# Fewer, larger groups of small matrix products between the large ones

## The chip, the cores and the metric

One core of one Trainium2 chip runs the whole kernel, in one launch. The metric is the device time in microseconds (us). PE is TensorE (with PEld for its weight loads), DVE VectorE, ACT ScalarE, POOL GpSimd, SP SyncE, which issues most DMAs.

## The reference

One layer of a hybrid backbone over 640 tokens: 512 "latent" tokens on a grid and 128 "context" tokens, width 2048, float32.

```python
def _layer(x, mod, s0, shift_fn, lp):
    sh1, sc1, g1, sh2, sc2, g2 = jnp.split(mod, 6, axis=-1)       # mod = silu(c) @ w_mod + b_mod  (adaLN)
    h = _rmsnorm(x, lp['norm1_g']) * (1.0 + sc1) + sh1
    p = h @ lp['w_in']                                            # 2048 -> 5408 columns
    o_a, s_fin = _rwkv7_bidir(shift_fn(p[..., :C_SHIFT], lp['mu_shift']), s0, lp)
    o_b = _chunk_gmlp(jax.nn.gelu(p[..., C_SHIFT:]), lp)          # 8 groups of 128 columns
    x = x + g1 * (jnp.concatenate([o_a, o_b], axis=-1) @ lp['w_out'])
    h = _rmsnorm(x, lp['norm2_g']) * (1.0 + sc2) + sh2
    ff = (jax.nn.silu(h @ lp['w_ffn_gate']) * (h @ lp['w_ffn_up'])) @ lp['w_ffn_down']
    return x + g2 * ff, s_fin
```

`_rwkv7_bidir` runs, for 16 heads of 64 columns and for both directions, `S = S*w + (S a) b^T + v k^T; y = S r` over the tokens; the kernel does it in chunks of 64 tokens. `_chunk_gmlp` is, per group, a layer norm of one half and a 128x128 product over the tokens of a chunk, times the other half.

## The kernel before

Three stages follow one another. **The input stage** multiplies by `w_in` and prepares the recurrence; **the second stage** runs the recurrence over the chunks, with the output projection (`wout`, L1081 to L1083) as filler; **the third** is the feed-forward part. Only the input stage's code is touched.

Every float32 product of the large matrices is made of three products of rounded halves, of 128x320 outputs each: in `win` L194 (`h_hi`,`hi`), L195 (`h_lo`,`hi`) and L198 (`h_hi`,`lo`); below, "large products". The input stage walks over 43 blocks of 128 columns of `w_in`, four pieces of 24 large products to a block. `wide` counts eighths of a piece; twice in each half of a piece `between` lets three `Mixer` queues trace some of the small work, up to a budget that each `yield` of that work spends: `mixA` (the blocks' own work: `take_r`, `take_v`, `take_k` for a pair of heads; `take_gv`, `take_gu` for a gMLP group), `mixS` (`solve`, a 16x16 substitution on DVE) and `mixM` (`merge`, which joins the 16x16 inverses of a pair into 64x64 ones). A negative yield ends the budget, an integer holds the queue. After the last block the queues are drained, and then whatever is left of `mod_all`, the adaLN products. What is traced so is placed on each engine by a list scheduler; only the first and second stage's PE order is written by hand. Each engine runs its instructions in the order placed.

The small products, all in the input stage:
- in `take_k`'s `chunks`, once for each of 8 pairs and 2 directions: `pG` (L677) in three groups, then transposes `pXT` (L697) in groups of 8 and of 2 chunks, then `pW` (L711) in two groups of 5 chunks. `both(name)` hands out the two PSUM banks g0 and g1 of pool `pk`, one buffer each, so that a new group waits until ACT or DVE has copied out the one before.
- in `merge`, for each pair and direction: three `pblk` groups (L885, 32x32 tiles), `pM` (L910) and `pT` (L919), each of them copied out before the next. Their PSUM tiles come from `pt_`, which has two buffers.
- `pvt`, `pw` (transposes) and `psp` of a gMLP group or of `take_v`, full 128x128, from `pt_` too.
- `pm` (L948): the adaLN products, 2x512 outputs, four of them side by side in four column strips of the array; `mod_all` loads 2 MB of `w_mod`, uses them in two times four products, and so on for 32 loads. One `next(mods)` is taken 1.36 times per piece. `mod_cols` (L180, `ptm`) transposes a finished part. The loads, and the sum with the bias (`ms`), use one SBUF slot (`mraw`) in turn.

The second stage's first work is `o_load` (L1067 to L1069): SP loads `ol` from the gMLP outputs in DRAM (`d_o`), ACT casts it to `oh`, DVE subtracts. These tiles lie over the input stage's released SBUF.

Of the kernel before, what the change touches and what calls it, by code (L numbers as in the profile page):

```python
# [49 lines left out]
MODR = 1.36  # L50
# [39 lines left out]
def flow_step(ctx: ExitStack, tc, x_prompt, x_sample, state_rwkv, c, c_ctx, w_mod, b_mod,  # L90
# [456 lines left out]
    def take_v(pr, p):  # L547
        o = pairs[p]
        o.zv = bk.tile([P, T], F32, tag="zv", name="zv", bufs=1)
        yield from shifted(o.zv, pr, 16 + p)  # L550
        yield 1.5
        vt = bp.tile([P, NT, P], F32, tag="vt", name="vt", bufs=1)
        for (t0, t1) in ((0, 4), (4, 5)):
            ps = pt_.tile([P, 4, P], F32, tag="pt", name="pvt")
            for t in range(t0, t1):
                TE.transpose(ps[:, t - t0, :], o.zv[:, t * P:(t + 1) * P], ident)
            S.copy(vt[:, t0:t1, :], ps[:, 0:t1 - t0, :])
            yield 0.5
        nc.sync.dma_start(d_vt[p, 0].rearrange("(q t) v -> t q v", t=P), vt)
        nc.sync.dma_start(c3(d_vt[p, 1]), c3(d_vt[p, 0])[:, ::-1])  # L560

    def take_k(pr, p):
# [104 lines left out]
        def chunks(d):  # L667
# [7 lines left out]
            for (c0, c1) in ((0, 4), (4, 8), (8, NCH)):  # L675
# [4 lines left out]
                    for cc in range(c0, c1) for h in range(2)])  # L680
# [14 lines left out]
            for (c0, c1) in ((0, 8), (8, NCH)):  # L695
                two = [ps.rearrange("p (c t) -> p c t", t=CH) for ps in both("pXT")]
                in_turn([lambda cc=cc, h=h: TE.transpose(  # L697
                    two[h][:, cc - c0, :], X[hsl(h), cc].rearrange("p s t -> p (s t)"), ident[hsl(h), hsl(h)])
                    for cc in range(c0, c1) for h in range(2)])
                for h in range(2):  # L700
                    ps = two[h]
                    XT = bz.tile([P, 8, CH], F32, tag="XT", name="XT", bufs=2)
                    S.copy(XT[:, 0:c1 - c0, :], ps[:, 0:c1 - c0, :])
                    nc.sync.dma_start(d_S[p, :, d, c0:c1, F_X + CH * h:F_X + CH * h + CH], XT[:, 0:c1 - c0, :])
                yield 0.2 * (c1 - c0)
            two = [ps.rearrange("p (c t) -> p c t", t=CH) for ps in both("pW0")]
            for c0 in (0, 5):
                ps = two[c0 // 5][:, 0:5, :]
                for cc in range(c0, c0 + 5):
                    for h in range(2):  # L710
                        TE.matmul(ps[osl(h), cc - c0, :], GA[hsl(h), cc, :], Z[hsl(h), cc, h, :], start=True, stop=True)  # L711
                for h in range(2):
                    S.copy(Z[osl(h), c0:c0 + 5, h, :], ps[osl(h)])
                yield 1.0
# [45 lines left out]
    def take_gv(vv, g):  # L760
# [10 lines left out]
        for (t0, t1) in ((0, 4), (4, 5)):  # L771
            ps = pt_.tile([P, 4, P], F32, tag="pt", name="pvt2")
            for t in range(t0, t1):
                TE.transpose(ps[:, t - t0, :], vv[:, t * P:(t + 1) * P], ident)
            S.copy(vt[:, t0:t1, :], ps[:, 0:t1 - t0, :])
            yield 0.6
# [25 lines left out]
    def take_gu(uu, g):  # L802
# [5 lines left out]
        for (t0, t1) in ((0, 4), (4, 5)):  # L808
            ps = pt_.tile([P, 4, P], F32, tag="pt", name="psp")
            for t in range(t0, t1):  # L810
                TE.matmul(ps[:, t - t0, :], vt[:, t, :], wspT, start=True, stop=True)
# [50 lines left out]
    def merge(p, d2):  # L862

        GB = pairs[p].GB
        for gq in range(8):
# [8 lines left out]
        yield HOLD  # L874
        for d in range(2):
            GBd = GB[d]
            TF = bp.tile([P, NCH, CH], F32, tag="TF", name="TF")
            Tn, TT, A1 = TB[:, d, :, 0, :], TB[:, d, :, 1, :], A1_[:, d]

            def blk(lhs, rhs, rows=range(4)):  # L880
                ps = pt_.tile([P, NCH, 32], F32, tag="pt", name="pblk")
                for cc in range(NCH):
                    for a_ in rows:
                        s = slice(32 * a_, 32 * a_ + 32)
                        TE.matmul(ps[s, cc, :], lhs[s, cc, :], rhs[s, cc, :], start=True, stop=True,  # L885
                                  tile_position=(32 * a_, 32 * a_))
                return ps

            M1 = bp.tile([P, NCH, 32], F32, tag="M1", name="M1")
            yield -1.0  # L890
            ps = blk(A1, Tn)
            S.copy(M1, ps)
            yield 1.6
            yield -1.0

            ps = blk(TT, M1, (0, 2))
            for h in range(2):
                V.tensor_add(Tn[lo32(h)], ps[lo32(h)], Tn[lo32(h)])
            yield 1.6
            yield -1.0  # L900
            ps = blk(M1, TT)
            V.tensor_add(TF[:, :, 32:64], ps, TT)
            S.activation(TF[:, :, 0:32], TF[:, :, 32:64], AF.Copy, scale=mlo[:, 0:1])
            yield 1.7
            M2 = bp.tile([P, NCH, 32], F32, tag="M1", name="M2")
            yield -1.0
            ps = pt_.tile([P, NCH, 32], F32, tag="pt", name="pM2")
            for cc in range(NCH):
                for h in range(2):
                    TE.matmul(ps[hi32(h), cc, :], GBd[lo32(h), cc, 32:64], Tn[lo32(h), cc, :],  # L910
                              start=True, stop=True, tile_position=(64 * (1 - h), 64 * (1 - h) + 32))
            for h in range(2):
                S.copy(M2[hi32(h), :, :], ps[hi32(h), :, :])
            yield 1.2
            yield -1.0
            ps = pt_.tile([P, NCH, 32], F32, tag="pt", name="pT2")
            for cc in range(NCH):
                for h in range(2):
                    TE.matmul(ps[lo32(h), cc, :], M2[hi32(h), cc, :], TF[hi32(h), cc, 32:64],  # L919
                              start=True, stop=True, tile_position=(64 * (1 - h) + 32, 64 * (1 - h)))  # L920
            for h in range(2):
                S.copy(TF[lo32(h), :, 32:64], ps[lo32(h), :, :])
            yield 1.2
            BQ.dma_start(d_S[p, :, d, :, F_T:F_T + CH], TF)
            merged.append(p)
        G.memset(TB[:, :, :, 0, 0:16], 0.0)


# [10 lines left out]
    def mod_all():  # L939
        for g in (2, 4, 3, 5):  # L940
            pm = cur["psum"].tile([P, 512], F32, tag="pmod", name=f"pm{g}")
            quad = load_mod(g, 0)
            for _ in range(4):
                yield
            for kb in range(0, KB, 2):
                for u in range(2):
                    for j in range(4):
                        TE.matmul(pm[32 * j:32 * j + 2, :], cT[:, 2 * (kb + u):2 * (kb + u) + 2], quad[:, u, j, :],  # L948
                                  start=(kb + u == 0), stop=(kb + u == KB - 1), tile_position=(0, 32 * j))
                for _ in range(2):  # L950
                    yield
                if kb + 2 < KB:
                    quad = load_mod(g, kb + 2)
                    for _ in range(4):
                        yield
# [6 lines left out]
            yield  # L962
            yield
            for j in range(4):
                V.tensor_add(ms[32 * j:32 * j + 2, :], pm[32 * j:32 * j + 2, :], ms[32 * j:32 * j + 2, :])
            mod_cols(cur["tp"], ms, modc[g], tag=cur["tag"])
            yield
# [25 lines left out]
    mods = mod_all()  # L993
    due = 0.0
# [26 lines left out]
    for n, (b, q) in list(enumerate(pieces))[N0:]:  # L1021
# [6 lines left out]
        due += MODR  # L1028
        while due >= 1.0:
            due -= 1.0  # L1030
            next(mods, None)
# [3 lines left out]
    for _ in mods:  # L1035
        pass
# [1134 lines left out]
```

## Time and profile before

| | |
|---|---|
| time, median of 3 runs | 3188.06 us (3185.64 to 3188.2) |
| the profiled execution: its time / its span | 3182.42 us / 3180.6 us |
| PE, weight loads, DVE, ACT, POOL busy | 96%, 89%, 74%, 46%, 39% |
| input stage, first to last large product | 49.5 to 1062.9 us of the span |
| TensorE clock granted, mean | 0.993 |

A row of the timeline gives the start in us of the span, the time from the group's first start to its last end, the engine, the code line, what is written from what, the sizes and the count; in brackets the idle time ahead of it and what ended that. A float32 product outside `win` shows as two records. The input stage is the first third of the span.

### The profile page before, as it was taken

Reading aid. Unit: us, or ns where it says so; the run is one execution under the profiler, and the core shown is the slowest. Engines: PE = TensorE matmul, PEld = TensorE weight load, DVE = VectorE, ACT = ScalarE, POOL = GpSimd, SP = SyncE. Lnnn points to the kernel's source line nnn. Section 1 sums busy time; section 2 is a strip of 40 time slices with the busy share of each in tenths; the row PEclk is TensorE's granted clock in tenths of the full one; section 3 lists DMA queues with packets and bytes.
Section 4 is the critical chain, followed back from the end, with each engine's and each line's share of the span. In section 5 each row is a group of like instructions: output and inputs, shape, how many; then the busy total and the mean of one; then the engine's idle time right before and its main releaser. Section 6 shows DMA issues by size and latency. Waiting matters only on the chain.

```text
span 3180.6 us, 71623 instructions
## 1 busy us (share of the span) xinstructions
PE 3059.6 (96%) x27896; PEld 2844.7 (89%) x27896; DVE 2354.6 (74%) x4119; ACT 1474.4 (46%) x3216; POOL 1238.2 (39%) x1081
## 2 busy tenths in 40 slices
PE   6999999999999999999999999999999999999997
PEld 3788878788878888899999999999999999999997
DVE  4567777667776688767977777777777787888888
ACT  3344544544454444357544444444444454444365
POOL 2001121221122034411456665666656645555542
PEclk9999999999999999999999999999999999999999
DMA  9767786867777688575343434434343364554453
GB/s 371 249 190 201 213 233 175 218 196 203 210 208 202 205 285 275 157 221 155 110 132 107 121 118 127 122 107 127 119 122 119 109 200 150 159 167 123 135 163 123
DMA packets 740436, 550.84 MB, mean 173 GB/s; under 512 B 141056, under 2 KB 673504, under 8 KB 731264
## 3 DMA queue, kind: packets, MB, share of 16 engines
q1 hardware_dynamic: 727136, 532.47, 55.4%
q0 software_dynamic: 10624, 13.23, 1.8%
q8 instruction: 219, 3.59, 0.5%
q14 instruction: 121, 0.99, 0.1%
q10 hardware_dynamic: 2336, 0.57, 0.1%
HBM read 437.79 MB, written 110.95 MB: 173 GB/s over the span
## 4 chain that ended last, share of the span: by engine, by line
PE 45%; DVE 3%; issue 1%; DMA 1%; POOL 1%; ACT 0%; SPq 0%; DVEq 0%; POOLq 0%; ACTq 0%
PE P L1688 15%; PE P L1685 15%; PE P L1686 15%; DVE lo L1466 1%; DMA opd<-d_op 0%; DVE xd L1754 0%; DMA x1d<-d_x 0%; POOL rawd L1594 0%; DVE cd L1944 0%; DMA rawd<-in_w_ffn_down_dram 0%; DVE out L2138 0%; DVE acc L1925 0%; ACT hi L1465 0%; DMA xd<-d_os 0%; POOL t L1594 0%
## 5 line engine op out<-in xcount | busy, mean ns | idle before, releaser
L1685 PE MATMUL P<-xo,hi 128*128 128x320 f32 x2352 | 699.3, 309 | 0.2 <-ACT hi L1465 0.2
L1686 PE MATMUL P<-xo,hi 128*128 128x320 f32 x2352 | 699.1, 309 | 0.0
L1466 DVE TENSOR_TENSOR lo<-raw,hi 128x512 fp32r<-128x512 f32 x526 | 513.0, 981 | 162.3 <-ACT hi L1465 159.8
L1465 ACT CAST hi<-raw 128x512 fp32r<-128x512 f32 x526 | 326.9, 622 | 466.4 <-PE P L1686 384.2
L1688 PE MATMUL P<-xo,lo 128*128 128x320 f32 x2352 | 440.8, 309 | 5.0 <-DVE lo L1466 5.0
L194 PE MATMUL big<-h_hi,hi 128*128 128x320 f32 x1376 | 438.4, 325 | 6.8 <-ACT hi L172 3.9
L1685 PEld LDWEIGHTS P<-xo,hi 128*128 128x128 f32 x2352 | 441.3, 188 | 0.5 <-ACT hi L1465 0.5
L1686 PEld LDWEIGHTS P<-xo,hi 128*128 128x128 f32 x2352 | 441.6, 188 | 0.0
L195 PE MATMUL big<-h_lo,hi 128*128 128x320 f32 x1376 | 423.1, 314 | 0.8 <-DVE h_lo L358 0.7
L1594 POOL TENSOR_TENSOR raw<-raw 128x512 f32<-128x512 f32 x252 | 410.2, 1637 | 10.1 <-DVE lo L1466 1.8
L1688 PEld LDWEIGHTS P<-xo,lo 128*128 128x128 f32 x2352 | 369.0, 188 | 6.0 <-DVE lo L1466 6.0
L1685 PE MATMUL P<-xd,hi 128*128 128x320 f32 x1232 | 367.7, 310 | 5.5 <-ACT hi L1465 2.3
L1686 PE MATMUL P<-xd,hi 128*128 128x320 f32 x1232 | 366.8, 309 | 0.0
L198 PE MATMUL big<-h_hi,lo 128*128 128x320 f32 x1376 | 320.1, 313 | 2.1 <-DVE lo L173 2.1
L194 PEld LDWEIGHTS big<-h_hi,hi 128*128 128x128 f32 x1376 | 261.9, 190 | 57.2 <-issue 25.3
L173 DVE TENSOR_TENSOR lo<-raw,hi 128x512 fp32r<-128x512 f32 x268 | 185.2, 694 | 156.1 <-ACT hi L172 154.4
L1594 POOL TENSOR_TENSOR t<-raw 128x512 f32<-128x512 f32 x84 | 125.1, 1490 | 425.3 <-DMA raw<-in_w_ffn_up_dram 362.0
L1465 ACT CAST hi<-rawd 128x512 fp32r<-128x512 f32 (+1 forms) x288 | 167.0, 585 | 225.3 <-PE P L1686 153.3
L172 ACT CAST hi<-raw 128x512 fp32r<-128x512 f32 x268 | 164.5, 618 | 223.2 <-PE big L195 86.1
L195 PEld LDWEIGHTS big<-h_lo,hi 128*128 128x128 f32 x1376 | 262.0, 190 | 5.8 <-DVE h_lo L358 1.9
L1466 DVE TENSOR_TENSOR lo<-rawd,hi 128x512 fp32r<-128x512 f32 (+1 forms) x288 | 241.3, 844 | 24.6 <-ACT hi L1465 24.3
L1688 PE MATMUL P<-xd,lo 128*128 128x320 f32 x1232 | 236.9, 310 | 7.2 <-DVE lo L1466 7.2
(406 smaller groups left out, 6085.4 us busy)
## 6 DMA issues: line engine op xcount, KB each, us to landing
wt<-in_w_mod_dram SPq DMA_DIRECT2D x96, 1024.0 KB
raw<-in_w_ffn_gate_dram SPq DMA_DIRECT2D x182, 256.0 KB
raw<-in_w_ffn_up_dram SPq DMA_DIRECT2D x182, 256.0 KB
rec<-d_S SPq DMA_DIRECT2D x80, 576.0 KB
raw<-in_w_in_dram SPq DMA_DIRECT2D x172, 256.0 KB
rawd<-in_w_ffn_down_dram SPq DMA_DIRECT2D x128, 256.0 KB
raw<-in_w_out_dram SPq DMA_DIRECT2D x96, 256.0 KB
xd<-d_os SPq DMA_DIRECT2D x66, 320.0 KB
```

The source lines that it names most:

```text
L172: S.copy(hi, raw)
L173: V.tensor_sub(lo, raw, hi.bitcast(F32))
L194: TE.matmul(halves[hf], hi[:, k, :], h_hi[:, kb, s], start=(kb == 0), stop=False)
L195: TE.matmul(halves[hf], hi[:, k, :], h_lo[:, kb, s], start=False, stop=False)
L198: TE.matmul(halves[hf], lo[:, j - 4 * q, :], h_hi[:, j, s], start=False, stop=(j == KB - 1))
L1465: S.copy(hi[:, 0:nk], raw[:, 0:nk])
L1466: V.tensor_sub(lo[:, 0:nk], raw[:, 0:nk], hi[:, 0:nk].bitcast(F32))
L1594: G.tensor_tensor(out=o[:, 0:nk], in0=p[:, 0:nk], in1=q[:, 0:nk], op=ALU.subtract)
L1685: TE.matmul(ps, hi[:, k, :], xk[:, 0, :], start=q == 0 and k == 0 and not filled, stop=False)
L1686: TE.matmul(ps, hi[:, k, :], xk[:, 1, :], start=False, stop=False)
L1688: TE.matmul(ps, lo[:, k, :], x(i, 4 * q + k)[:, 0, :], start=False, stop=q == nq - 1 and k == nk - 1 and last)
```

## The change

1. **XT and W.** `chunks` still makes 8 chunks' transposes in one group; the last two chunks' transposes go into spare columns of the two `pW` banks, and all ten chunks' W products follow at once.
2. **Merge.** The five steps are done for both directions at once: two PSUM tiles (both buffers of `pt_`), two groups of products, then both copies. The result is built in place in `TB` instead of `TF`; `TB` is cleared as a whole ahead of a pair's loads on POOL, not in part after it.
3. **Transposes and psp.** The groups of 4 and 1 tiles become one of 5, in two PSUM tiles.
4. **adaLN.** `mod_all` now yields distances in eighths of a piece: 18 from a load to its products, 8 after them. When the products are due, `site`, called behind several small groups, has them traced at once and queued behind that group's last product (`tc.issue_after`); when none has come within 8 more eighths they are traced as before.
5. The first `pG` group of each call takes its heads in the other order.

```diff
-MODR = 1.36
+MODL, MODU, MODX = 18, 8, 8
...
@@ chunks
-            for (c0, c1) in ((0, 8), (8, NCH)):
-                two = [ps.rearrange("p (c t) -> p c t", t=CH) for ps in both("pXT")]
...
-            two = [ps.rearrange("p (c t) -> p c t", t=CH) for ps in both("pW0")]
-            for c0 in (0, 5):
...
+            two = [ps.rearrange("p (c t) -> p c t", t=CH) for ps in both("pXT")]
+            turn(two, 0, 8)
+            turned(two, 0, 8)
+            yield 1.6
+            two = [ps.rearrange("p (c t) -> p c t", t=CH) for ps in both("pW")]
+            last = [ps[:, 5:7, :] for ps in two]
+            turn(last, 8, NCH, (1, 0))
+            for cc in range(NCH):
+                for h in range(2):
+                    mm = TE.matmul(two[cc // 5][osl(h), cc % 5, :], GA[hsl(h), cc, :], Z[hsl(h), cc, h, :],
+                                   start=True, stop=True)
+            site(mm.ins)
+            turned(last, 8, NCH)
...
@@ merge
+        if p:
+            G.memset(TB, 0.0)
...
+        two, (_, mm) = zip(*(blk(A1[d], Tn[d]) for d in range(2)))
+        site(mm)
         for d in range(2):
-            GBd = GB[d]
-            TF = bp.tile([P, NCH, CH], F32, tag="TF", name="TF")
...
+            S.copy(M1[d], two[d])
+        yield 3.2
+        yield -1.0
+        two, _ = zip(*(blk(TT[d], M1[d], (0, 2)) for d in range(2)))
...
+        for d in range(2):
+            BQ.dma_start(d_S[p, :, d, :, F_T:F_T + CH], TB[:, d].rearrange("p c w b -> p c (w b)"))
             merged.append(p)
-        G.memset(TB[:, :, :, 0, 0:16], 0.0)
...
@@ mod_all
             for kb in range(0, KB, 2):
+                cur["loose"] = True
+                yield MODL
+                cur["loose"] = False
+                with cur.pop("after", None) or ExitStack():
...
+                yield MODU
...
+    def mods_on(late):
+        while cur["mods"] and wide[0] >= cur["due"] + (late if cur["loose"] else 0):
+            n = next(cur["mods"], None)
...
+    def site(ins):
+        if cur["mods"] and cur["loose"] and wide[0] >= cur["due"]:
+            cur["after"] = tc.issue_after(ins)
+            cur["due"] = wide[0] + next(cur["mods"])
...
-        due += MODR
-        while due >= 1.0:
-            due -= 1.0
-            next(mods, None)
+        mods_on(MODX if n < 7 * len(pieces) // 8 else 0)
...
-    for _ in mods:
+    for _ in cur["mods"] or ():
         pass
```

How the placed order changes, at three places. PE in the first pair's forward direction, from the first group of transposes on, before (the rows at "..." are large products; L697 are the transposes, L711 the W products):

```order
L697 MATMUL pXT<-ident,X 128x64 x16
...
L697 MATMUL pXT<-ident,X 128x64
...
L697 MATMUL pXT<-ident,X 128x64 x3
...
L711 MATMUL pW_2073<-Z,GA 64x64 x10
...
L711 MATMUL pW_2074<-Z,GA 64x64 x10
```

and after (L716 are the W products, L969 the adaLN products):

```order
L697 MATMUL pXT<-ident,X 128x64 x16
...
L697 MATMUL pW<-ident,X 128x64 x4
L716 MATMUL pW<-Z,GA 64x64 x20
L969 MATMUL pm_1191<-wt,cT 2x512 x8
L198 MATMUL big<-h_hi,lo 128x320
```

Five groups became two, and one load of adaLN products stands behind the second.

PE at the end of the input stage, before (L811 `psp`, L767 `pw` and L774 `pvt` are the last two gMLP groups' products, L1338 transposes of x, L1081 to L1083 the output projection's large products):

```order
L919 MATMUL pT_13397<-TF,M_13342 32x32 x20
L811 MATMUL psp<-wspT,vt_12993 128x128 x4
L1081 MATMUL big<-oh,hi 128x320
...
L774 MATMUL pvt_13453<-ident,praw 128x128 x4
...
L1081 MATMUL big<-oh,hi 128x320 x2
...
L811 MATMUL psp<-wspT,vt_13452 128x128 x5
```

and after (L820, L776, L782 are the same three; L180 the last adaLN part's transposes; L1170 the recurrence's first products; L1110 and L1111 the output projection):

```order
L198 MATMUL big<-h_hi,lo 128x320 x2
L820 MATMUL psp<-wspT,vt_12944 128x128 x5
L1367 MATMUL pxT<-ident,x1T 128x128 x4
L776 MATMUL pw<-ident,wsp 128x128
L782 MATMUL pvt_13387<-ident,praw 128x128 x4
L782 MATMUL pvt_13388<-ident,praw 128x128
L1367 MATMUL pxT<-ident,x1T 128x128 x16
L820 MATMUL psp<-wspT,vt_13386 128x128 x5
L180 MATMUL ptm<-ident,ms_13347 128x128 x4
L1170 MATMUL swap<-I_68,s_13508 64x64 x4
L1110 MATMUL big<-oh,hi 128x320 x2
L1111 MATMUL big<-ol,hi 128x320
```

No large product stands between `pvt` and the last `psp` any more; the output projection begins behind both.

SP's DMA queue at the same place, before (L1067 are the output projection's operands, L818 the write of a finished gMLP group, L1127 and L1132 the recurrence's operands):

```order
L1067 DMA ol<-d_o 128x640 x4
L171 DMA raw<-in_w_out_dram 128x4x128
L1127 DMA rec<-d_S 128x2x576 x2
L804 DMA bsp<-in_b_spatial_dram 128x128
L1127 DMA rec<-d_S 128x2x576
L818 DMA d_o<-praw 128x640
L1127 DMA rec<-d_S 128x2x576
```

and after (L978 is the last adaLN part's bias, L829 the write of a group, L1096 the operands):

```order
L978 DMA ms_13347<-in_b_mod_dram 1x512 x8
L829 DMA d_o<-praw 128x640
L814 DMA bsp<-in_b_spatial_dram 128x128
L1156 DMA rec<-d_S 128x2x576 x4
L1161 DMA s_13508<-in_state_rwkv_dram 128x2x64
L1161 DMA s_13510<-in_state_rwkv_dram 128x2x64
L1156 DMA rec<-d_S 128x2x576
L829 DMA d_o<-praw 128x640
L1096 DMA ol<-d_o 128x640 x4
```

The four operand loads moved from ahead of the last two groups' writes to behind both. The first of them now also waits for a product on PE; in the order before it waits for none. From the recurrence's first chunk on (`w_ps`), PE's order is the same as before to the end of the program.

More of the change, by code (lines that the diff above doesn't have):

```diff
@@ L911, in merge @@
                               start=True, stop=True, tile_position=(64 * (1 - h), 64 * (1 - h) + 32))
+        for d in range(2):
             for h in range(2):
[L913 to L916, printed above, removed]
+                S.copy(M2[d][hi32(h), :, :], two[d][hi32(h), :, :])
+        S.activation(TB[:, :, :, 0, :], TB[:, :, :, 1, :], AF.Copy, scale=mlo[:, 0:1])
+        yield 2.4
@@ L917, in merge @@
+        yield -1.0
+        two = [pt_.tile([P, NCH, 32], F32, tag="pt", name="pT2") for d in range(2)]
+        for d in range(2):
             for cc in range(NCH):
                 for h in range(2):
[L919 removed]
+                    TE.matmul(two[d][lo32(h), cc, :], M2[d][hi32(h), cc, :], TT[d][hi32(h), cc, :],
                               start=True, stop=True, tile_position=(64 * (1 - h) + 32, 64 * (1 - h)))
+        for d in range(2):
```

136 lines of the change are left out of this document (66 added, 70 removed).

## The prediction

> **What bounds the kernel now.** I read the page's first parts, then the table by stage, then the timeline of PE.
>
> ```profile
> span 3180.6 us, 71623 instructions
> PE 3059.6 (96%) x27896; PEld 2844.7 (89%) x27896; DVE 2354.6 (74%) x4119; ACT 1474.4 (46%) x3216; POOL 1238.2 (39%) x1081
> core 0: us, PE busy (x) PEld busy (x) DVE busy (x) ACT busy (x) POOL busy (x), PEclk, DMA share, GB/s
> 49.50:160.00 110.50, 100.89 (x646) 74.11 (x647) 54.28 (x126) 35.06 (x60) 1.74 (x2) 0.94 0.83 284
> 160.00:1062.90 902.90, 869.45 (x10586) 746.46 (x10587) 621.83 (x1229) 438.21 (x933) 157.83 (x258) 0.99 0.73 201
> 1062.90:1090.00 27.10, 24.68 (x211) 22.13 (x210) 22.27 (x42) 15.51 (x30) 2.15 (x2) 1.00 0.86 286
> ```
>
> PE is the bound, in the touched stage too: it stands still for 902.90 - 869.45 = 33.45 us there, DVE is at 69%, and the DMA engines are not full. So two things can move the time: how long PE needs for its stream, and how long it stands still. Moved work on the other engines counts only through the second.
>
> **The price of a small group.** The timeline of PE around three groups of the first pair:
>
> ```profile
> 224.52 0.45 PE L198 MATMUL big<-h_hi,lo 128*128 128x320 f32 x2
> 224.91 0.27 PE L697 MATMUL pXT<-ident,X 64*128 64x64 f32 x1
> 225.11 0.42 PE L194 MATMUL big<-h_hi,hi 128*128 128x320 f32 x1
> 225.37 0.31 PE L195 MATMUL big<-h_lo,hi 128*128 128x320 f32 x1
> ...
> 228.61 0.31 PE L194 MATMUL big<-h_hi,hi 128*128 128x320 f32 x1
> 228.76 0.31 PE L195 MATMUL big<-h_lo,hi 128*128 128x320 f32 x1
> 228.90 0.31 PE L198 MATMUL big<-h_hi,lo 128*128 128x320 f32 x1
> 229.14 0.80 PE L711 MATMUL pW<-Z,GA 64*64 64x64 f32 x20
> 229.87 0.42 PE L198 MATMUL big<-h_hi,lo 128*128 128x320 f32 x1
> 230.13 0.31 PE L194 MATMUL big<-h_hi,hi 128*128 128x320 f32 x1
> ...
> 373.97 0.66 PEld L711 LDWEIGHTS pW<-Z,GA 64*64 64x64 f32 x20 [0.19 <-issue]
> ```
>
> Large products follow each other every 0.147 us (228.61, 228.76, 228.90). A small group breaks that three times. The step into it takes 0.24 (228.90 to 229.14), 0.09 too much. The first large product behind it takes 0.26 (229.87 to 230.13), 0.11 too much. And the group's last product, whose turn inside the group would be some 0.03 (20 loads in 0.66), holds PE until it has run out; 229.14 to 229.87 is 0.73, 19 turns of 0.03 are 0.58, so 0.15, that is 0.12 too much. Together 0.31 us that carry no work. The smallest group shows it alone: from the second product at 224.67 (the row holds two) to 225.37 there are two large products and one transpose in 0.70 us; less 2 x 0.147 and the 0.03, 0.37. I take 0.31, with 0.28 and 0.37 as ends. Joined behind a group of another kind, a group saves the 0.09 and the 0.11 alone.
>
> Groups of full 128x128 transposes have another price:
>
> ```profile
> 256.53 0.31 PE L195 MATMUL big<-h_lo,hi 128*128 128x320 f32 x1
> 256.68 0.27 PE L774 MATMUL pvt<-ident,praw 128*128 128x128 f32 x1
> 256.70 0.53 PE L198 MATMUL big<-h_hi,lo 128*128 128x320 f32 x2
> 257.08 0.31 PE L194 MATMUL big<-h_hi,hi 128*128 128x320 f32 x1
> ```
>
> From 256.53 to 257.08 lie three large products and one transpose: 0.55 - 3 x 0.147 = 0.11, its own turn. Joining `pvt` and `psp` saves nothing, and adaLN products behind them save nothing over standing alone.
>
> **The count.** In the placed order of the input stage PE steps from large or full-size products into a group of smaller tiles 234 times before and 150 times after; with changes of kind inside a group, groups of one kind fall from 295 to 206: merge 97 to 52, transposes 48 to 32, W 32 to 16, `pG` 56 to 44, adaLN 61 to 62. So 84 x 0.31 + 5 x 0.11 = 26.6 us. adaLN itself:
>
> ```profile
> 300.20 1.90 PE L948 MATMUL pm<-wt,cT 128*2 128x512 f32 x16
> 506.13 1.02 PE L948 MATMUL pm<-wt,cT 128*2 128x512 f32 x2
> 507.57 1.89 PE L948 MATMUL pm<-wt,cT 128*2 128x512 f32 x14
> ```
>
> Four products run side by side; one alone (x2) costs 1.02, about as much as four, so a group that the scheduler cuts other than at four pays some 0.86 more. There are 13 such cuts before and 12 after: other large or small products still slip between the first product, which alone is tied, and the rest. That part of the change gives 0.9 us. Sum of the stream: -27.5 us, between -24 (0.28) and -32 (0.37).
>
> [...]
>
> **The end of the stage.** Here I expect the change to lose. Before, the output projection starts as soon as the last large product of the input stage is done, because its operands are loaded ahead:
>
> ```profile
> 1057.54 1.92 SPq L1067 DMA_DIRECT2D ol<-d_o  x4
> 1060.60 0.73 ACT L1068 CAST oh<-ol 128x640 fp32r<-128x640 f32 x1
> 1069.90 0.73 ACT L1068 CAST oh<-ol 128x640 fp32r<-128x640 f32 x1
> 1063.54 1.16 PE L811 MATMUL psp<-wspT,vt 128*128 128x128 f32 x8
> 1064.46 0.39 PE L1081 MATMUL big<-oh,hi 128*128 128x320 f32 x1
> 1066.12 0.49 PE L811 MATMUL psp<-wspT,vt 128*128 128x128 f32 x2 [1.27 <-ACT TF L922]
> 1067.29 0.82 PE L774 MATMUL pvt<-ident,praw 128*128 128x128 f32 x5
> 1079.94 1.38 PE L811 MATMUL psp<-wspT,vt 128*128 128x128 f32 x10 [0.78 <-DVE vt L798]
> 1083.24 0.33 SPq L818 DMA_DIRECT2D d_o<-praw  x1
> ```
>
> The last gMLP group's chain (transposes at 1067.29, norm on DVE, ACT and POOL, `psp` at 1079.94, its write at 1083.24) runs for 20.3 us behind the last large product (1062.9) while PE works on the projection. Afterwards the adaLN products end some 90 eighths of a piece later, beside the last pieces; the bias, sum and transposes that follow keep the slot `mraw` until the drain. The operand loads wait for a product on PE, which I read as those last transposes (they lie over that slot), and stand on SP behind the last group's write. So nothing covers the chain, and then the loads come too.
>
> Counted from the last large product: the chain 20.3, less some 2.5 because DVE does not do the projection's sums between (18); the loads 3.06 until the first cast (1057.54 to 1060.60), the cast 0.73: the first projection product at 22, against 1.6 before. In that time PE does what it did before between the large products: 10 `psp`, 6 transposes, 20 transposes of x, the bias' 4, `swap`, with 0.11 each for the single ones and 1.1 for five `psp`: 6 us. Idle 16, and 2 more until all four operands are there; before, this place had 27.10 - 24.68 = 2.4 idle. Loss 15.6. And the clock:
>
> ```profile
> 324.60:327.50 2.90, 0.29 (x2) 0.03 (x1) 2.82 (x5) 0.62 (x1) 0.00 (x0) 1.00 0.13 38
> 329.20:332.60 3.40, 3.40 (x65) 3.07 (x63) 3.24 (x9) 1.31 (x3) 0.00 (x0) 0.50 0.94 307
> ```
>
> A wait of 2.65 us is followed by 3.4 us at half clock (column PEclk): 1.7 us lost. One such dip belongs to the new gap. [...]
>
> Loss at the end: 17 us. Ends: 10, if the chain without any large product beside it takes 13 instead of 18; 25, if it takes the full 20.3 and the four loads come as slowly as before under load.
>
> **Waits elsewhere.** In the stage PE waits most for these:
>
> ```profile
> PE pG L677 <- DVE GA L689: 8.1, 8, 2.4
> PE pG L677 <- DVE mix L848: 3.8, 1, 3.8
> PE ptm L180 <- issue: 3.1, 2, 2.6
> PE pW L711 <- ACT XT L703: 2.3, 2, 2.0
> PE pT L919 <- ACT M L913: 1.2, 4, 0.5
> ```
>
> The `pG` waits stay: the groups' copies and DVE's load are not touched, and their number is chance. One turn of the banks g0 and g1 per `chunks` call goes (of the 2.3 for XT, a part), and `ptm` gets a distance to the sum it reads (3.1). Against that, every merge step now holds both tiles of `pt_`, and whatever needs one stands on PE until both copies are done. I take -2, between -10 and +10 of the 33.45. ACT and DVE do the same copies, fewer by a handful. On POOL the clearing of `TB` waits for the write of the pair before and holds POOL's DMAs behind it; POOL is busy 157.83 of 902.90 us there and nobody on PE waits for it by name: nothing. The loads of `w_mod` come 26 to 34 eighths apart instead of 35: within the DMA share of 0.73, nothing.
>
> **Sum.** -27.5 + 17 - 2 = -12.5 us. The profiled execution took 3182.42, so 3170 in its terms; the median of the runs stands 5.6 us above it, and 3188.06 - 12.5 = 3175.5. A measurement here tells about 0.2%, 6.4 us, from no change.
>
> **Rivals.**
> - *The end is covered after all* (the scheduler's order is followed, but the chain is much shorter, or the loads wait for an earlier product and the large products are late by little). For it: DVE is free there. Against: SP's order, in which the loads stand behind the last write, can't be overtaken. Without the loss: -27.5 - 2 + 2 = -27.5, 3160.5. Chance 0.12.
> - *The gain is eaten at the end*: loss of 25 and the waits no better: -27.5 + 25 + 1, 3186.5. For it: the loads took 10 us for all four before (cast 1060.60 to the fourth at 1069.90). Against: then other loads ran beside them. Chance 0.13.
> - *The two tiles of `pt_`* become a queue: 8 pairs times 5 joined steps, each with a wait w behind it on PE, since the next group in PE's order often needs a tile whose copy has not run. It decides the sign at 12.5 / 40 = 0.31 us, and makes the kernel slower by more than 0.2% at 0.47. For it: `psp` in the tail waited 1.27 us for such a copy before. Against: before, `pT` waited for its copies just 1.2 us in all, and the scheduler knows of the tiles. At 0.5 us: 3188.06 - 12.5 + 20 = 3195.5. Chance 0.07.
>
> **How the numbers follow.** The first case, 3175.5, has 0.68; its own range is -20 to -6. The rest is above. The range leaves out the ends of the two outer rivals: 3161 to 3190. Faster by over 0.2%: 0.68 x 0.9 + 0.12 = 0.73; within 0.2%: 0.07 + 0.13 = 0.20; slower: 0.07.
>
> **What would show it.** In the profile afterwards: the last large product of the input stage near 1062.9 - 29 = 1034; 16 rows of W with 40 records instead of 32 with 20; merge groups of 160, 80, 160, 80, 80 records; the first projection product about 22 us behind the last large one, with PE idle for most of it and a dip of the clock behind. If that gap is under 10 us, the loss is wrong; if the stage ends later than 1045, the price of a group or the waits are.

## The result, and the profile after

The changed kernel takes 3203.40 us (median of 6 runs) against 3187.16 us for the kernel before beside it: ratio 1.0060, interval 1.0048 to 1.0072. By the medians it is 16 us slower, by the ratio 19, where 12.5 us less was forecast.

The profiled execution of after took 3199.67 us. Its page, and its table by stage (from to, length, busy time of PE, PEld, DVE, ACT, POOL, granted clock, DMA share):

```profile
span 3197.9 us, 71565 instructions
PE 3051.6 (95%) x27896; PEld 2851.3 (89%) x27896; DVE 2348.7 (73%) x4119; ACT 1473.4 (46%) x3208; POOL 1245.6 (39%) x1080
...
49.50:160.00 110.50, 100.92 (x646) 74.14 (x647) 54.01 (x126) 35.13 (x60) 1.74 (x2) 0.94 0.80 274
160.00:1061.80 901.80, 852.31 (x10618) 745.96 (x10617) 617.80 (x1222) 437.15 (x926) 164.91 (x258) 0.98 0.73 202
1061.80:1089.00 27.20, 15.21 (x67) 10.65 (x66) 18.25 (x31) 12.02 (x24) 1.18 (x1) 0.58 0.63 209
```

The last large product comes at 1061.8 against 1062.9: the input stage gained 1.1 us, not 29. PE worked 17.1 us less there (852.31 against 869.45) and stood still 49.49 us instead of 33.45, 16.0 more. The clock column hides a second loss: the time at half clock between 160 us and the stage's end rose from 17.1 to 44.4 us; I count half of such time as lost, 22.2 instead of 8.5. So by subtraction the stream itself became 1.1 + 16.0 + 13.7 = 31 us shorter.

The groups look as forecast: 16 rows of W and XT with 44 records, 150 entries into small groups. A merge group of 160 records costs 1.6 us when nothing disturbs it (the first below). Two others, from PE's timeline of the same execution:

```profile
974.04 0.45 PE L198 MATMUL big<-h_hi,lo 128*128 128x320 f32 x2
974.43 1.64 PE L895 MATMUL pblk<-TB,M 32*32 32x32 f32 x160
976.00 0.42 PE L194 MATMUL big<-h_hi,hi 128*128 128x320 f32 x1
...
823.66 1.44 PE L895 MATMUL pblk<-TB,A__1117 32*32 32x32 f32 x130
827.41 0.61 PE L895 MATMUL pblk<-TB,A__1117 32*32 32x32 f32 x28 [2.31 <-issue]
...
845.73 1.50 PE L895 MATMUL pblk<-TB,M 32*32 32x32 f32 x150
849.84 0.31 PE L895 MATMUL pblk<-TB,M 32*32 32x32 f32 x10 [2.61 <-issue]
```

PE stops in the middle of a group, at its 130th or 150th record, with no semaphore behind the wait ("issue"). The table of the first wait and of what follows it, and the DMA queue that carries PE's instructions (packets, MB, share), show what happens:

```profile
824.90:827.40 2.50, 0.20 (x18) 0.08 (x10) 2.46 (x5) 0.64 (x2) 0.00 (x0) 1.00 1.06 257
827.50:830.90 3.40, 3.40 (x44) 1.47 (x47) 3.40 (x6) 1.93 (x4) 0.00 (x0) 0.50 0.97 193
```

```profile
q8 instruction: 219, 3.59, 0.4%
...
q8 instruction: 1, 0.02, 1.5%
```

The first q8 row is the whole run's: 219 packets, 3.59 MB, 16 KB each. PE has 2 x 27,896 loads and products and 392 waits of its own, 56,184 instructions, so a packet brings 256 of them (56,184 / 219 = 256.5), that is some 128 products. The number of packets follows PE's instructions in other kernels too: 207 for 52,997 in m2_merge_half, 239 for 61,324 in d1_double (both below), 256.0 and 256.6 to a packet. The second q8 row is 824 to 828 us: one such packet, started at 825.07, landed at 826.00, and PE went on at 827.41. I call a PE gap over 0.35 us a supply stall when it begins at the end of a block of 256 (numbers 192 to 195 of the count modulo 256) and ends 1.15 to 1.7 us behind such a packet. After has nine in the stage, 15.8 us, six of them 1.35 to 2.8 us long; before has one of 0.6. These gaps run from the start of one weight load to the start of the next and so hold a product's own turn; of the profile's idle time they are 12.4 us in after and 0.4 in before. The place in the block is not only my definition: of the 107 waits of PE over 0.35 us that read "issue" in this stage, in all kernels of this document, 82 begin there, and 23 of the other 25 stand ahead of `ptm`. The second table row is the half clock that follows (0.50).

How soon a block is used up is one half of it. In four of the nine, 3.4 to 3.9 us lie between the start of the block and that of the next (667.4, 823.7, 845.9, 1029.5 us); the shortest block of before took 4.1 us. The other half is when the packet starts: two of the nine end blocks of 6.8 and 6.4 us (from 442.2 and 974.9 us), and there the packet started only 4.3 and 4.1 us after the block; at the one stall of before it was 4.4 us, in six others of after 0.8 to 2.5. A block of 2.9 us (from 531.9 us) went by without a wait. Why a packet starts late is not shown.

The rest of the idle time grew less: 49.5 - 12.4 = 37.1 us against 33.4 - 0.4 = 33.0. From the list for 160 to 1036 us of after:

```profile
PE pG L678 <- DVE mx L861: 11.4, 3, 4.9
PE pblk L895 <- issue: 8.0, 5, 2.6
PE pXT L697 <- DVE GA L690: 5.6, 8, 1.8
PE pXT L697 <- DVE modc L1506: 3.6, 1, 3.6
PE pG L678 <- DVE GA L690: 1.9, 3, 1.1
```

Before, `pG` waited 8.1 + 3.8 us for DVE; now 11.4 + 1.9, while DVE works through `solve` (`mx`).

The end of the stage, from PE's, SP's and ACT's timeline:

```profile
1077.66 2.50 PE L820 MATMUL psp<-wspT,vt 128*128 128x128 f32 x10 [3.44 <-DVE vt L808]
1080.56 1.08 PE L180 MATMUL ptm<-ident,ms 128*128 128x128 f32 x4 [0.40 <-issue]
1085.78 0.90 PE L1110 MATMUL big<-oh,hi 128*128 128x320 f32 x2 [3.52 <-ACT oh L1097]
...
1081.58 0.34 SPq L829 DMA_DIRECT2D d_o<-praw  x1
1082.02 1.85 SPq L1096 DMA_DIRECT2D ol<-d_o  x4
...
1085.01 0.72 ACT L1097 CAST oh<-ol 128x640 fp32r<-128x640 f32 x1 [7.37 <-DMA ol<-d_o]
```

This is the forecast chain: last `psp`, last adaLN transposes, last write, operand loads, cast, first projection product 24.0 us behind the last large one. But PE's part in it is not the forecast one: in the 27.2 us of the table it stood idle for 12.0, and the clock was at half for 23.9 us from 1066.4 us on (0.58 on average in the table, 1.00 before). From the last large product to the second stage's first products of the next kind (L1524 before, L1553 after) it took 296.3 us before and 313.7 now.

### The profile page after: what moved, and what is told of

Same layout as the page of the kernel before. It is cut to its first block, busy times and chain, and to the rows that moved or that the text cites. A ratio compares the mean times of both kernels' runs of the same rounds, so it can differ in the third digit from the quotient of the medians.

```text
span 3197.9 us, 71565 instructions
## 1 busy us (share of the span) xinstructions
PE 3051.6 (95%) x27896; PEld 2851.3 (89%) x27896; DVE 2348.7 (73%) x4119; ACT 1473.4 (46%) x3208; POOL 1245.6 (39%) x1080
## 3 DMA queue, kind: packets, MB, share of 16 engines
q8 instruction: 219, 3.59, 0.4%
## 4 chain that ended last, share of the span: by engine, by line
PE 45%; DVE 2%; DMA 1%; issue 1%; POOL 1%; ACT 0%; SPq 0%; DVEq 0%; POOLq 0%; ACTq 0%
PE P L1717 15%; PE P L1714 15%; PE P L1715 15%; DVE lo L1495 1%; DMA rawd<-in_w_ffn_down_dram 0%; DMA opd<-d_op 0%; DVE xd L1783 0%; DMA x1d<-d_x 0%; POOL rawd L1623 0%; DVE cd L1973 0%; DVE out L2167 0%; POOL t L1623 0%; DVE acc L1954 0%; PE P L2107 0%; DMA xd<-d_os 0%
## 5 line engine op out<-in xcount | busy, mean ns | idle before, releaser
L1495 DVE TENSOR_TENSOR lo<-rawd,hi 128x512 fp32r<-128x512 f32 (+1 forms) x288 | 229.2, 802 | 27.2 <-ACT hi L1494 27.1
## 6 DMA issues: line engine op xcount, KB each, us to landing
raw<-in_w_ffn_gate_dram SPq DMA_DIRECT2D x182, 256.0 KB
raw<-in_w_ffn_up_dram SPq DMA_DIRECT2D x182, 256.0 KB
raw<-in_w_in_dram SPq DMA_DIRECT2D x172, 256.0 KB
rawd<-in_w_ffn_down_dram SPq DMA_DIRECT2D x128, 256.0 KB
raw<-in_w_out_dram SPq DMA_DIRECT2D x96, 256.0 KB
```

What stands on the lines that cost most here:

```text
L1495: V.tensor_sub(lo[:, 0:nk], raw[:, 0:nk], hi[:, 0:nk].bitcast(F32))
```

## The experiments

Theory A: PE's instructions come in blocks of 256 (219 packets for 56,184 of them, above). A run of over a hundred tiny products uses most of a block up in 1.2 us (111 in 1.19 us from 450.99 us of after); then the next is not there, PE stands (1.67 us there), and the clock drops (0.50 from 455.4 us). Theory B, the forecast's third rival: with both tiles of `pt_` held, PE waits for copies. The columns from "stage end" on come from one profiled execution each, which lies up to 11 us from its kernel's median (s1_split 11 and t1_early 8 above it; a1_adaln 8, a2_nosite 6 and m1_merge 5 below), so small differences between them say nothing: end of the input stage, gap to the first projection product, supply stalls (by the gaps as above), PE's idle time and half the half-clock time, the last three from 160 us to the stage's end. The kernels with "half" in their names leave out every second chunk's own left block in the merge; their results are not the layer's, and they serve to measure alone.

| kernel | median / before beside it, us | ratio, interval | stage end | gap | stalls | idle | clock loss |
|---|---|---|---|---|---|---|---|
| before | | | 1062.9 | 1.6 | 0.6 | 33.4 | 8.5 |
| after | 3203.4 / 3187.2 | 1.0060, 1.0048-1.0072 | 1061.8 | 24.0 | 15.8 | 49.5 | 22.2 |
| m1_merge | 3207.8 / 3185.8 | 1.0073, 1.0051-1.0095 | 1083.8 | 0.9 | 17.7 | 50.7 | 20.5 |
| m2_merge_half | 3182.4 / 3184.8 | 0.9993, 0.9981-1.0006 | 1056.9 | 0.9 | 1.3 | 38.4 | 8.5 |
| d1_double | 3253.4 / 3185.8 | 1.0214, 1.0192-1.0236 | 1135.9 | 1.6 | 44.8 | 63.1 | 27.3 |
| s1_split | 3198.0 / 3185.8 | 1.0046, 1.0029-1.0063 | 1083.9 | 0.9 | 12.4 | 62.2 | 35.8 |
| t1_early | 3211.0 / 3185.8 | 1.0077, 1.0050-1.0105 | 1095.1 | 0.9 | 26.3 | 68.0 | 32.4 |
| t3_last | 3195.4 / 3185.1 | 1.0036, 1.0023-1.0049 | 1072.9 | 0.9 | 16.3 | 55.7 | 30.7 |
| h1_half | 3180.2 / 3184.2 | 0.9983, 0.9972-0.9994 | 1037.2 | 24.3 | 0.0 | 40.4 | 15.4 |
| h2_half_early | 3190.5 / 3184.2 | 1.0024, 1.0009-1.0038 | 1069.8 | 0.9 | 0.5 | 60.8 | 18.8 |
| h4_half_last | 3168.7 / 3185.1 | 0.9946, 0.9932-0.9960 | 1049.9 | 0.9 | 0.0 | 51.1 | 18.8 |
| h3_both_half | 3174.3 / 3184.8 | 0.9976, 0.9963-0.9988 | 1050.5 | 0.9 | 0.0 | 42.4 | 17.1 |
| j1_joins | 3188.5 / 3184.8 | 1.0013, 1.0000-1.0026 | 1062.2 | 0.9 | 11.6 | 55.6 | 13.7 |
| a1_adaln | 3236.9 / 3185.1 | 1.0161, 1.0145-1.0176 | 1087.7 | 24.6 | 1.8 | 50.6 | 22.2 |
| a2_nosite | 3201.2 / 3184.8 | 1.0054, 1.0033-1.0076 | 1052.6 | 29.4 | 1.9 | 27.8 | 1.7 |
| n1_untied | 3206.3 / 3182.2 | 1.0076, 1.0059-1.0093 | 1066.0 | 26.3 | 12.2 | 51.3 | 18.8 |
| x1_xtw | 3176.9 / 3184.2 | 0.9981, 0.9967-0.9995 | 1055.1 | 1.6 | 2.5 | 40.0 | 10.2 |
| x1_again | 3177.8 / 3185.1 | 0.9979, 0.9968-0.9991 | 1055.2 | 1.6 | 0.7 | 39.0 | 13.7 |
| b1_best | 3182.2 / 3184.2 | 0.9986, 0.9975-0.9996 | 1056.4 | 0.9 | 0.0 | 41.6 | 11.9 |
| x2_free | 3190.0 / 3183.7 | 1.0023, 1.0011-1.0034 | 1067.9 | 1.6 | 5.3 | 38.3 | 18.8 |

**The joined merge alone (m1_merge): before, with the merge of the diff and nothing else.**

> The kernel before with the joined merge alone; the rest, adaLN too, as before. Theory A (instruction supply: PE's instructions come in blocks of 256, that is of 128 products, and a run of 160 tiny products uses a block up in 1.5 us, faster than the next is fetched, so PE stands inside the group with 'issue' as its reason; a dip of the clock follows): the stream gains 45 x 0.31 = 14 us, some six stalls of 2.2 us cost 13 and their dips 7, so 3 to 9 us slower than before, no gain, and the new waits are inside or just behind groups of 160 records and read 'issue'. Theory B (both tiles of pt_ are held, PE waits for the slowest copy): about the same time, but the new waits carry the names of ACT or DVE copies (M, TB) ahead of the merge groups. If the joined merge is not what costs: 14 us faster.

It loses 22 us, more than expected, and its timeline shows the same picture:

```profile
651.79 1.37 PE L884 MATMUL pblk<-TB,A__1117 32*32 32x32 f32 x132
655.30 0.44 PE L884 MATMUL pblk<-TB,A__1117 32*32 32x32 f32 x28 [2.14 <-issue]
```

**The same merge with half the instructions (m2_merge_half).**

```diff
-            for cc in range(NCH):
+            for cc in range(0, NCH, 2):
...
-                    mm = TE.matmul(ps[s, cc, :], lhs[s, cc, :], rhs[s, cc, :], ...
+                    mm = TE.matmul(ps[s, cc:cc + 2, :], lhs[s, cc, :], rhs[s, cc:cc + 2, :], ...
```

> The kernel before with the joined merge alone, and in its first three steps one chunk's left block against two chunks' right blocks (left out: every second chunk's own left block). Against the joined merge alone (22 us slower than before) only the number of instructions falls; tiles, copies and waits are the same. Theory A: the 17.7 us of supply stalls go, and most of the 12 us of clock behind them; the products themselves are 6 us shorter: 3174 to 3184. Theory B (both tiles of pt_ held): 6 us less than the joined merge, 3202.

25 us come back. Tiles, copies and waits are the same as in m1_merge; the products' own time is 6 us less (1.32 instead of 1.62 us for each of 16 groups, 1.31 instead of 1.45 for each of 8). The stage by the table, m1_merge's first, then m2_merge_half's: PE stands still 50.7 and 38.4 us.

```profile
160.00:1083.80 923.80, 873.12 (x10622) 752.73 (x10621) 620.75 (x1229) 435.01 (x925) 162.83 (x257) 0.98 0.71 196
```

```profile
160.00:1056.90 896.90, 858.46 (x9035) 738.02 (x9034) 619.72 (x1229) 438.13 (x927) 163.90 (x258) 0.99 0.74 203
```

Theory B falls: it asked for 3202. Against before, though, the joined merge without stalls gains nothing clear of noise (0.9981 to 1.0006): its idle time is 5.0 us above before's.

**More instructions in the kernel before (d1_double).** Each product of the first and third merge step is issued twice: `for a_ in rows * 2`.

> The kernel before, in which each product of the first and third merge step is issued twice (the same product into the same place), so that these 32 groups have 160 records instead of 80; no wait, tile, copy or pool is different. The doubled work itself is 32 x 80 x 9.4 ns = 24 us. Theory A: stalls inside these groups with 'issue' as their reason, in about six of sixteen as in the changed kernel, so 12 x 2.2 = 26 us and up to 20 us for clock dips on top: 50 to 70 us slower than before. Theory B: nothing is waited for that wasn't before: 24 us slower, with no stall inside the groups.

68 us slower, 24 of them the doubled work; 25 supply stalls of 44.8 us in place of one. No wait or tile differs from before. The longest is inside a merge group:

```profile
594.01 0.74 PE L885 MATMUL pblk<-TB,A__1117 32*32 32x32 f32 x62
599.22 0.26 PE L885 MATMUL pblk<-TB,A__1117 32*32 32x32 f32 x2 [4.47 <-issue]
```

**Half the instructions in the changed kernel (h1_half).** The same edit as in m2_merge_half.

> The changed kernel, in which a product of the merge's first three steps takes one chunk's left block against two chunks' right blocks (32x64 outputs), so that these groups have 80 and 40 records instead of 160 and 80; left out: every second chunk's own left block. Tiles, copies, waits, adaLN and the tail stay as they are. Theory A (instruction supply): a run no longer uses up a block of 256 instructions faster than the next one comes, so the supply stalls of the input stage fall from 15.8 us to under 5, half-clock time behind them falls too, and the kernel is 12 to 20 us faster than the changed one: 3183 to 3191. Theory B (PE waits for copies because both tiles of pt_ are held): those waits are all still there, within 5 us of the changed kernel.

23 us faster than the changed kernel, 6 of them again the shorter products. A whole group, from the timeline, and the stage, from the table:

```profile
827.58 1.32 PE L895 MATMUL pblk<-TB,M 32*32 32x64 f32 x80
```

```profile
160.00:1037.20 877.20, 836.84 (x9012) 731.39 (x9011) 614.91 (x1221) 437.15 (x926) 163.87 (x258) 0.98 0.76 207
```

The stage ends at 1037.2, 25.7 us earlier than before; the gap of 24 us stays.

**Groups of 160 cut into two (s1_split).** `two = zip(*(blk(...) for d ...))` becomes a loop over the directions with the copy and a `yield` in each turn, for the first and third step.

> The changed kernel with the two groups of 160 records of each merge (first and third step) traced as two of 80 again, one per direction; all else stays. Theory A: 16 entries more cost 5 us, but the stalls inside the groups (13 us) and their clock dips (some 7) go: 15 us less than the changed kernel, near 3188, and the input stage ends near 1047. Theory B: two of five joined steps are cut, so two fifths of the 26 us of new waits, less 5 for the entries: 5 us less than the changed kernel.

The gain over the changed kernel is 5 us, B's number, but stalls of 12.4 us remain. That two groups of 80 stand so close that they still use up a block together was my guess; it was not shown. As a test between A and B it failed. Its gap at the end is 0.9 us, so adaLN's end moved too, and its profiled execution is 11 us above its median, so its row says little on the stage.

**adaLN ends earlier (t1_early, h2_half_early).** `MODL, MODU, MODX = 16, 6, 8`, in the changed kernel and in h1_half.

> The changed kernel with the adaLN distances 16 and 6 instead of 18 and 8 eighths, so that adaLN ends well before the last large product. If the tail is held by the adaLN transposes and by the operand loads that wait for them, the first projection product comes 1.6 to 3 us behind the last large one as before, and the kernel is 17 us faster than the changed one (3186). If the tail has another cause (order of the scheduler, the last gMLP group itself), the gap stays near 24 us and the time near 3203.

> The same with adaLN's distances 16 and 6 instead of 18 and 8; left out: every second chunk's own left block in the merge. Theory A: neither the supply stalls nor the gap of 24 us behind the last large product are left, so the stream's gain of 27 us shows at last: 3160 to 3172. If the run with 16 and 6 was slow for another reason (adaLN closer together, loads of w_mod late), this one stays above 3190 too. Theory B: as the run with 16 and 6, near 3205.

The gap goes, as forecast (0.9 us), and yet neither is faster than with 18 and 8: h2_half_early is 10 us slower, t1_early 8 by the medians (the intervals overlap). The loads of `w_mod` are closer together; from the DMA issues of 320 to 600 us and the waits of 160 to 1036 us, h1_half first, then h2_half_early:

```profile
wt<-in_w_mod_dram SPq DMA_DIRECT2D x17, 1024.0 KB
...
PE big L194 <- ACT hi L172: 4.9, 4, 2.3
```

```profile
wt<-in_w_mod_dram SPq DMA_DIRECT2D x24, 1024.0 KB
...
PE big L194 <- ACT hi L172: 14.8, 7, 4.4
PE pm L969 <- DMA wt<-in_w_mod_dram: 3.9, 3, 1.4
```

The large products wait 10 us more for their weights and adaLN 3.9 for its own. That the closer loads cause the 10 us is not shown: ACT, which prepares these weights, waits no longer for the loads of `w_in` (32.6 us in h2_half_early, 34.9 in h1_half). In t1_early the stalls also take 26.3 us, against 15.8 in after.

**Only the last adaLN part earlier (t3_last, h4_half_last).** `yield (14 if g == 5 else MODL)`, in the changed kernel and in h1_half.

> The changed kernel with a distance of 14 instead of 18 eighths for the last of the four adaLN parts alone, so that adaLN ends about ten pieces' worth of small steps before the last large product, while the rest of the stage keeps its pace. If the late adaLN alone makes the tail: the first projection product comes 1 to 3 us behind the last large one (24 before), and the kernel is 14 to 19 us faster than the changed one: 3184 to 3189, since the supply stalls stay. If the run with 16 and 6 showed that ending early itself costs as much: no gain, near 3203.

> The kernel with half the merge records (every second chunk's own left block is left out) and the distance of 14 eighths for the last adaLN part. If instruction supply and late adaLN are all that ate the stream's gain, both are gone here: the stage ends near 1043 with the projection right behind it, 3160 to 3168. If the loss in the run with half the records and the distances 16 and 6 came from ending early, and not from loads of w_mod that are closer together, it is 3180 or more.

The gap goes without closer loads over the whole stage. Against the kernels without this edit the gain is 8 us for t3_last and 11.5 us for h4_half_last, less than the 17 that the gap seemed to cost: the chain's own products lie inside the stage again, and idle time there rises by 6.2 and 10.7 us. h4_half_last is 16.4 us faster than before, some 6 of them the shorter products. So with the stalls and most of the end out some 10 us of the change are left; idle time and clock loss are still 17.7 and 10.3 us above before's.

**The joins without the late adaLN (j1_joins; h3_both_half).** The first is the changed kernel with before's `mod_all`; the second is before with the XT and W join and m2_merge_half's merge.

> The changed kernel with adaLN left as before (1.36 steps a piece, nothing tied behind a group): the joined groups alone. Theory A (instruction supply): no gap at the end, but the supply stalls stay (12 to 26 us by where the blocks of 256 fall) and their clock dips: 3185 to 3205, with at least five stalls over 1.2 us inside or just behind groups of 160 records. If the joins are sound and adaLN is what costs: 3160 to 3170.

> The kernel before with XT and W joined and with the joined merge in half the instructions (left out: every second chunk's own left block), adaLN as before. Theory A: the XT and W part's 7 us on top of the run with the merge in half the instructions: 3167 to 3177, with less than 3 us of supply stalls, and no gap at the end.

The joins alone win nothing (8 stalls, 11.6 us); with half the merge instructions, 8 (by the ratio) to 10.5 us (by the medians), 6 of them the shorter products.

**adaLN alone (a1_adaln, a2_nosite), and the changed kernel without the tie (n1_untied).** `site` returns at once in the last two.

> The kernel before with the adaLN part alone (distances 18 and 8, products behind a small group where one comes). No group is joined, so no supply stalls beyond before's; the stage within 3 us of before's, the projection some 20 us behind the last large product: 14 to 19 us slower than before, 3200 to 3205. If the tail comes only with the joined groups: the same as before, 3186.

> The kernel before with adaLN's distances of the change (18, 8, and 8 more), but its products never tied behind a small group. If the tie is what cost 25 us inside the input stage when adaLN was changed alone: the stage ends within 6 us of before's and only the gap at the end stays, 3200 to 3206. If the new distances cost it: as that run, 3230 to 3240.

> The changed kernel, in which adaLN's products are never tied behind a small group (they are traced when due and 8 eighths late). If the tie costs the changed kernel what it cost where adaLN was changed alone (36 us between the runs with and without it): 3165 to 3175, with the supply stalls of the joined groups still there. If that cost belonged to the unjoined groups alone: within 8 us of the changed kernel, 3195 to 3211.

The gap at the end appears in all three, with nothing joined too, so it belongs to the late adaLN. But a1_adaln also lost 25 us inside the stage, which neither theory expected; without the tie that is gone (a2_nosite ends the stage 10 us before the kernel before). In the changed kernel taking the tie out changes nothing that can be measured. The waits in the two kernels with adaLN alone, a1_adaln first and then a2_nosite:

```profile
PE pG L679 <- DVE GA L691: 11.9, 9, 3.1
PE pwa L607 <- ACT tha L611: 8.6, 4, 4.6
PE pW L713 <- ACT XT L705: 6.9, 7, 2.2
```

```profile
PE pG L679 <- DVE GA L691: 2.6, 4, 0.9
PE pwa L607 <- ACT tha L611: 2.6, 4, 0.8
PE pW L713 <- ACT XT L705: 3.3, 7, 1.2
```

Why the tie makes DVE and ACT late in the one kernel and not in the other stays open.

**The one part that wins (x1_xtw, x1_again), and two tries to add to it.** The first two are before with `turn`, `turned` and the joined W of the diff, without `site`. b1_best adds the merge with its groups of 160 cut as in s1_split; x2_free adds the untied adaLN with 14 eighths for its last two parts.

> The kernel before with the joined XT and W groups alone. Theory A: the longest run grows to 44 records, far under the 128 of a block, so no new supply stalls; 16 W groups and 16 transposes are saved, 16 x 0.31 + 16 x 0.2 = 8 us faster than before: 3178, the input stage ending near 1055. Theory B (a joined group waits for its slowest piece): W now waits for Z as well as for GA and XT's banks at once; no gain, 3186 to 3190.

> The kernel before with the joined XT and W groups alone, once more and in more rounds, since it is the one correct part that gained: again 4 to 9 us faster than before, 3177 to 3182, if the 32 groups saved are worth 8 us and no supply stall is added; equal to before if the first time was chance.

> The kernel before with XT and W joined and with the merge of both directions at once, its groups of 160 records cut into two of 80; adaLN as before. Theory A: longest run 80 records, but two of them close together can still use up a block: 3 or 4 supply stalls, 8 us; 29 + 32 entries fewer are worth 9 + 8 us; no gap at the end: 3170 to 3182. Theory B: the merge's waits for both tiles stay: 3186 to 3195.

> The parts that gained, in one correct kernel: the kernel before with XT and W joined, and adaLN with the change's distances but never tied behind a group, the last two of its four parts with 14 instead of 18 eighths so that it ends before the last pieces. XT and W are worth 7 us; the untied adaLN ended the input stage 10 us earlier in the run without the tie. If both hold and the gap at the end is gone: 3168 to 3175. If the 10 us came only because adaLN's last part was pushed behind the stage: 3176 to 3180, as with XT and W alone.

XT and W alone give 7 us twice (0.9981 and 0.9979; 8 were expected), and beat both kernels. b1_best wins 2 to 4 us, no more than XT and W alone: no stalls, but only 13 entries fewer (182 against 195, 4 us), which idle time and clock took back. x2_free missed: it was 10 us ahead of before at 953 us and 3 us behind at 997. In between lies no large supply stall (its one of 3.5 us is at 835.6), but a wait of 3.8 us of a large product for its weights from ACT (976.9) and 10.2 us of half clock behind it.

## Why the prediction was wrong

- **The stream, -27.5:** right, as far as subtraction shows it: 31 us in the changed kernel for 84 entries fewer, within the forecast's 24 to 32. The same subtraction gives 8 us for 30 entries fewer in m1_merge and 16 us for 39 fewer in x1_xtw. In h1_half the stage does end 25.7 us earlier, with 6 us of shorter products and, against that, 7 us more idle time and 7 more of clock loss.
- **The end of the stage, +17:** right in place and chain, and in size (17.4; the gap 24.0 instead of 22). The make-up of the 17 was wrong: 12.0 us of idle time instead of 18, and 23.9 us at half clock where one dip of 3.4 was put. That the sum agrees so well is in part luck. And it can't all be had back: 8 to 12 us.
- **Waits elsewhere, -2, between -10 and +10:** this step failed. PE's idle time rose by 16.0 us, 12.0 of it supply stalls, and the clock, which the forecast left out of the stage, took 13.7 more. The step looked for waits behind semaphores and took a longer group to cost only more of the same turns; that the instructions themselves have to arrive was not in it. Three of the eleven dips of the clock follow a supply stall directly, 5.1 us; the others follow waits of PE for DVE and ACT. So the stalls explain 17 of the 30 us, which agrees with what h1_half gave back (23 less the 6 of its shorter products). The other 13 stay open: idle time outside the stalls lies above before's 33.0 us in every kernel with joined groups (35.7 in m1_merge, 37.1 in after, 39.1 in x1_xtw, 46.0 in j1_joins), so part of what the joins save may turn into longer waits for other engines. But a1_adaln, with nothing joined, has 49.4 as well, and no run takes these apart.
- **The third rival**, the two tiles of `pt_`, came nearest in number (3195.5), but its mechanism is not what happened: m2_merge_half keeps both tiles held and loses nothing against before.
- **adaLN, 0.9:** its tie can't be seen in the changed kernel, where the run without it is equal within the intervals.
- The check named, "if the stage ends later than 1045, the price of a group or the waits are" wrong, pointed to the right term.

## To carry to other kernels

Joining small groups saved the step into and out of them (31 us for 84 entries fewer here, by subtraction), but count instructions as well as groups: here groups of 80 tiny products cost 0.6 us of supply stalls in the kernel before, and groups of 160 cost 15.8. Fewer, larger products were worth more than a longer run (25 us in m2_merge_half and 23 in h1_half, in each some 6 of them the shorter products); large products between two halves of a group left no stall in b1_best and 12.4 us in s1_split. "Issue" waits inside a group are worth counting against PE's instruction number before any semaphore is blamed: 82 of the 107 over 0.35 us here began at the end of a block. A background load that is moved late has to be followed to what its buffer holds up behind the stage (here the gap grew from 1.6 to 24.0 us); moving all of its loads closer together, so that it ended earlier, gained nothing here.

## What the runs showed of the hardware

- PE's instructions arrive in packets of 256 (219 packets of 16 KB for 56,184 instructions in the changed kernel), and the supply stalls begin at the same place of the block: at number 193 or 194 of the count modulo 256 in all nine of the changed kernel and in the one of the kernel before. They took 0.6 us in the kernel before, where no block of the stage was shorter than 4.1 us, 15.8 us in the changed kernel, and 44.8 us where the products were doubled (d1_double).
- Supply stalls of 1.67 us of idle time (from 452.2 us) and 2.31 us (from 825.1) were each followed by 3.4 us of half clock (from 455.4 and 827.5 us), and stalls of 2.09 and 1.60 us (from 979.2 and 1031.4) were not. So the length of a wait alone did not decide it here: one of 1.67 us brought a dip, and a longer one of 2.09 us none.
